# A batched 64x64 matrix product: half of seven result tiles leaves by another DMA queue, in three pieces

## The chip, the cores and the metric

The kernel runs on one core of a Trainium2 chip. A core has a matrix engine (TensorE, PE in the profile), a vector engine (VectorE, DVE), a scalar engine (ScalarE, ACT), a general-purpose engine (GpSimd, POOL) and an engine that mostly issues transfers (SyncE, SP). Transfers between the main memory (HBM) and the on-chip memory are run by 16 DMA engines; SyncE, ScalarE and GpSimd each have a DMA queue of their own (q1, q10 and q0 in the profile). The metric is the device time of one execution in microseconds; the median of 3 runs before the change is 134.86 us (134.75 to 134.9).

## The reference

```python
def setup_inputs():
    return {
        "a": np.random.randn(1024, 64, 64).astype(np.float32),
        "b": np.random.randn(1024, 64, 64).astype(np.float32),
    }

def reference(a, b):
    return np.matmul(a, b).astype(np.float32)
```

There are 1024 independent products of two 64x64 matrices. Each input is 16.8 MB and so is the output.

## The kernel before

The 1024 products are worked off in 16 tiles of 64 products; t is the number of the tile, from 0 to 15. For one tile, b is 1.05 MB and the result is 1.05 MB. The matrix a is read in pieces for two tiles at a time; s is the number of such a piece, from 0 to 7.

The loads are these. `load_b(t)` (L93) issues one transfer, by SyncE for even t and by ScalarE for odd t, into one of 3 buffers. `load_a(s)` (L69) issues three transfers by GpSimd that convert to bf16 on the way (`a_sb`, 0.52 MB read each) and one by SyncE (`a_raw`, 0.52 MB). The first piece of a is loaded by SyncE and ScalarE.

The computation of a tile has these steps. `regroup(s)` (L99) puts the piece of a into another order on VectorE. `transpose(s, j)` (L115) turns it on TensorE and copies the result out on ScalarE (`at_sb`, L123). `spread(t)` (L128) makes the block-diagonal operand from it with four VectorE copies (`at_bd`, L133). `cast(t)` (L140) makes bf16 of the tile of b on VectorE (`b_bf`, L144). `multiply(t)` (L158) runs 64 matrix products in two halves and copies each half from PSUM into `o_sb` (L177), four copies a half: all on ScalarE, except that in odd tiles two of the eight are VectorE's. `o_sb` has 8 buffers, the PSUM tile `o_ps` has 2.

The result of tile t is handed to `store(t)` one tile later, after `multiply(t + 1)`. For t from 0 to 13 this is one transfer of the whole tile by GpSimd (L166); tile 14 goes out in two halves by SyncE and tile 15 in four quarters by SyncE and ScalarE.

The order of the work is written out by hand in the main loop (L229 to L256), and every engine and every DMA queue follows it in order. In the round of tile t the loop calls, in this order: `spread(t+1)`, `cast(t+1)`, `load_b(t+3)`, in some even rounds `load_a`, `transpose`, then `multiply(t)`, `regroup`, `transpose`, and `store(t-1)`. An engine that waits before it issues a transfer does nothing else meanwhile; for ScalarE this means that its copies (L123, L177) stand behind the issue of an odd tile of b.

One thing is not in the source but in the built program. Every transfer that SyncE or ScalarE issues signals its landing on one of eight semaphores, H0 to H7, taken in turn over both engines in program order; GpSimd's transfers have eight of their own. Before a transfer is issued, its engine waits until the transfer that last used the same semaphore has landed, unless another wait has made that sure already. So the ninth such transfer waits for the first, besides what its data and its buffer make it wait for.

Of the kernel before, what the change touches and what calls it, by code (L numbers as in the profile page):

```python
# [13 lines left out]
def kernel(  # L14
# [14 lines left out]
    nc = tc.nc  # L29
# [12 lines left out]
    o_v = out.rearrange("(t gh x) (mo w) n -> t (x mo) gh (w n)", gh=8, x=8, w=4)  # L42
# [19 lines left out]
    held = {}  # L62

    def store_queue(t, lo):
        if t < n_t - 2:
            return nc.gpsimd
        return nc.scalar if t == n_t - 1 and lo % 4 == 0 else nc.sync
# [90 lines left out]
    def multiply(t):  # L158
        at_bd = bd_tiles[t % N_BD][:].rearrange("p j g wl h mo -> p j g (wl h mo)")
        at_bd = at_bd.bitcast(bf16).rearrange("p j g (c u) -> p j g c u", u=2)  # L160
        b_bf = bbf_tiles.pop(t)
        last = t == n_t - 1
        o_sb = o_pool.tile([128, 8, 2, 2, 64], fp32, name="o_sb")

        def put(lo, n):
            store_queue(t, lo).dma_start(  # L166
                out=o_v[t, :, lo : lo + n, :],
                in_=o_sb[:, lo : lo + n].rearrange("p gh j wl n -> p (gh j wl n)"),
            )

        def evacuate(o_ps, gh, n, copies):

            for par in range(2):
                for wl in range(2):
                    src = o_ps[64 * wl : 64 * wl + 64, :, par, :, :]
                    dst = o_sb[64 * par : 64 * par + 64, gh : gh + n, :, wl, :]
                    copies[2 * par + wl](dst, src)  # L177

        for half in range(2):
            if not last:  # L180
                o_ps = o_psum.tile([128, 4, 2, 2, 64], fp32, name="o_ps")
            for g8 in range(8):
                if last and g8 % 4 == 0:
                    o_ps = t_psum.tile([128, 2, 2, 2, 64], fp32, name="at_ps")
                g = 8 * half + g8
                gl = (g8 % 4 if last else g8) // 2
                for j in range(2):
                    for u in range(2):
                        nc.tensor.matmul(  # L189
                            o_ps[:, gl, g % 2, j, :],  # L190
                            at_bd[:, j, g, :, u],
                            b_bf[:, g, 64 * u : 64 * u + 64],
                            start=(u == 0),
                            stop=(u == 1),
                        )
                if last and g8 % 4 == 3:
                    copy = nc.scalar.copy if g8 == 3 else nc.vector.tensor_copy
                    evacuate(o_ps, g // 4 * 2, 2, [copy] * 4)
            if not last:
                copies = [nc.scalar.copy] * 4  # L200
                if half and t % 2:
                    copies[2:] = [nc.vector.tensor_copy] * 2
                evacuate(o_ps, 4 * half, 4, copies)
        if last:
            held[t] = [lambda q=q: put(2 * q, 2) for q in range(4)]
        else:
            whole = t < n_t - 2
            held[t] = [lambda q=q: put(q, 8 if whole else 4) for q in ([0] if whole else [0, 4])]

    with tc.manual_schedule():  # L210
# [18 lines left out]
        for t in range(n_t):  # L229
            s, half = t // 2, t % 2  # L230
            if t + 1 < n_t:
                spread(t + 1)
                cast(t + 1)
            if t + B_AHEAD < n_t:
                load_b(t + B_AHEAD)
            if half == 0 and 0 < s < n_s - 1 - A_AHEAD:
                load_a(s + 1 + A_AHEAD)
            if half == 0 and 0 < s < n_s - 1:
                transpose(s + 1, 1)
            multiply(t)  # L240
            if t == 0:
                regroup(1)
                load_a(A_AHEAD)
                load_a(A_AHEAD + 1)
                transpose(1, 0)
                transpose(1, 1)
            elif t == 1:
                regroup(2)
            elif half == 0 and s + 2 < n_s:
                regroup(s + 2)  # L250
            if half == 1 and s + 2 < n_s:
                transpose(s + 2, 0)
            if t >= HOLD - 1:
                store(t - HOLD + 1)
# [32 lines left out]
```

## Time and profile before

| | us |
|---|---|
| median of 3 runs | 134.86 |
| span of the profiled execution | 133.1 |
| VectorE busy | 94.5 (71%) |
| ScalarE busy | 87.8 (66%) |
| TensorE busy | 65.7 (49%) |
| GpSimd busy | 33.7 (25%) |
| mean DMA rate by bytes written | 338 GB/s |
| HBM traffic over the span | 33.55 MB read, 16.78 MB written, 378 GB/s |

The profile covers one execution, whose span from the first to the last instruction is 133.1 us. The difference of 1.76 us to the median lies outside this span. Where a transfer converts to bf16, the rate counts the bytes written, which are half of those read. A page of the profile gives the busy time of the engines in 40 slices of the span; further views list the chain of work that ended last, the instructions in order of time, and for a transfer the time from its issue to its landing.

### The profile page before, as it was taken

Reading aid. Unit: us, or ns where it says so; the run is one execution under the profiler, and the core shown is the slowest. Engines: PE = TensorE matmul, PEld = TensorE weight load, DVE = VectorE, ACT = ScalarE, POOL = GpSimd, SP = SyncE. Lnnn points to the kernel's source line nnn. Section 1 sums busy time; section 2 is a strip of 40 time slices with the busy share of each in tenths; the row PEclk is TensorE's granted clock in tenths of the full one; section 3 lists DMA queues with packets and bytes.
Section 4 is the critical chain, followed back from the end, with each engine's and each line's share of the span. In section 5 each row is a group of like instructions: output and inputs, shape, how many; then the busy total and the mean of one; then the engine's idle time right before and its main releaser. Section 6 shows DMA issues by size and latency. Waiting matters only on the chain.

```text
span 133.1 us, 2837 instructions
## 1 busy us (share of the span) xinstructions
PE 65.7 (49%) x1152; PEld 62.7 (47%) x1152; DVE 94.5 (71%) x120; ACT 87.8 (66%) x161; POOL 33.7 (25%) x43
## 2 busy tenths in 40 slices
PE   0005504990068386059519672986199361776000
PEld 0005304980068275058509562975199360766000
DVE  5930299208999719598999699969999994978100
ACT  3134505899128999919899759696969987099600
POOL 8981000420082072143144022203020410210000
PEclk9999999999559999968996875579756985556855
DMA  3999999999999999999999999999999999999991
GB/s 75 367 332 311 307 312 279 278 307 326 328 307 402 316 322 334 393 385 401 318 282 365 402 397 356 308 307 387 395 396 387 393 396 391 402 403 402 380 339 41
DMA packets 19021, 45.01 MB, mean 338 GB/s; under 512 B 1088, under 2 KB 3136, under 8 KB 19008
## 3 DMA queue, kind: packets, MB, share of 16 engines
q0 software_dynamic: 6832, 20.19, 50.2%
q1 hardware_dynamic: 7120, 14.68, 30.5%
q10 hardware_dynamic: 5056, 9.96, 19.8%
q8 instruction: 9, 0.15, 0.4%
q14 instruction: 4, 0.03, 0.1%
HBM read 33.55 MB, written 16.78 MB: 378 GB/s over the span
## 4 chain that ended last, share of the span: by engine, by line
DMA 54%; DVE 18%; ACT 13%; issue 4%; PE 3%; SPq 1%; DVEq 0%; ACTq 0%
DMA b_sb<-in_b_dram 54%; ACT o_sb L177 9%; DVE at_bd L133 9%; DVE b_bf L144 4%; DVE o_sb L177 3%; PE at_ps L120 2%; ACT at_sb L123 2%; ACT b_bf L144 1%; PE o_ps L189 1%; DVE a_bf L108 1%; SPq L90 1%; DVE a_bf L111 1%; ACT b_bf L151 1%; SPq L96 0%; DVEq L133 0%
## 5 line engine op out<-in xcount | busy, mean ns | idle before, releaser
L177 ACT COPY o_sb<-o_ps 64x512 f32<-64x512 f32 x106 | 61.6, 581 | 9.5 <-PE o_ps L189 8.2
L189 PEld LDWEIGHTS <-at_bd 128*128 128x128 bf16 x1024 | 42.5, 113 | 39.7 <-DVE b_bf L144 26.8
L189 PE MATMUL o_ps<-b_bf,at_bd 128*128 128x64 bf16 x960 | 41.2, 213 | 36.0 <-DVE b_bf L144 25.1
L133 DVE COPY at_bd<-at_sb 32x1024 f32<-32x1024 f32 x64 | 46.6, 728 | 13.6 <-ACT at_sb L123 11.8
L120 PE MATMUL at_ps<-identity,a_bf 128*128 128x128 f32 x128 | 22.5, 350 | 19.3 <-ACT a_bf L105 11.4
L166 POOL DMA_DIRECT2D out_dram<-o_sb x14 | 16.3, 1166 | 55.4 <-ACT at_sb L123 23.0
L120 PEld LDWEIGHTS at_ps<-identity,a_bf 128*128 128x128 f32 x128 | 20.7, 190 | 19.4 <-issue 19.4
L144 DVE CAST b_bf<-b_sb 128x2048 bf16<-128x2048 f32 x14 | 17.5, 1249 | 10.0 <-DMA b_sb<-in_b_dram 9.8
L123 ACT COPY at_sb<-at_ps 128x512 f32<-128x512 f32 x32 | 17.4, 590 | 9.9 <-PE at_ps L120 7.6
L73 POOL DMA_DIRECT2D a_sb<-in_a_dram x21 | 13.3, 650 | 27.3 <-DVE a_bf L108 20.4
L177 DVE COPY o_sb<-o_ps 64x512 f32<-64x512 f32 x14 | 9.7, 690 | 0.3
L108 DVE COPY a_bf<-a_sb 128x3072 bf16<-128x3072 bf16 x7 | 7.4, 1059 | 0.0
L105 ACT CAST a_bf<-o_sb 128x1024 bf16<-128x1024 f32 x2 | 2.1, 1044 | 5.3 <-DMA o_sb<-in_a_dram 5.3
L111 DVE CAST a_bf<-a_raw 128x1024 bf16<-128x1024 f32 x7 | 4.8, 683 | 0.0
L144 ACT CAST b_bf<-b_sb 128x2048 bf16<-128x2048 f32 x1 | 1.9, 1897 | 4.1 <-DMA b_sb<-in_b_dram 4.1
L177 DVE COPY o_sb<-at_ps 64x256 f32<-64x256 f32 x8 | 3.4, 422 | 1.3 <-PE at_ps L189 1.2
L105 DVE CAST a_bf<-o_sb 128x1024 bf16<-128x1024 f32 x2 | 2.6, 1296 | 2.4 <-DMA o_sb<-in_a_dram 2.3
L189 PE MATMUL at_ps<-b_bf,at_bd 128*128 128x64 bf16 x64 | 3.6, 242 | 1.0 <-DVE at_bd L133 1.0
L217 DVE MEMSET at_bd<- 128x4096 f32 x1 | 3.5, 3472 | 0.8 <-issue 0.8
L151 ACT CAST b_bf<-b_sb 128x512 bf16<-128x512 f32 x2 | 1.1, 615 | 4.3 <-DMA b_sb<-in_b_dram 4.3
L177 ACT COPY o_sb<-at_ps 64x256 f32<-64x256 f32 x8 | 2.9, 367 | 0.1
L214 ACT ACT_TABLE_LOAD x1 | 1.3, 1283 | 2.3 <-issue 2.3
(12 smaller groups left out, 6.1 us busy)
## 6 DMA issues: line engine op xcount, KB each, us to landing
out_dram<-o_sb POOLq DMA_DIRECT2D x14, 1024.0 KB, 22.3
a_sb<-in_a_dram POOLq DMA_DIRECT2D x21, 256.0 KB, 16.4
a_raw<-in_a_dram SPq DMA_DIRECT2D x7, 512.0 KB, 19.1
o_sb<-in_a_dram SPq DMA_DIRECT2D x2, 512.0 KB, 6.2
o_sb<-in_a_dram ACTq DMA_DIRECT2D x2, 512.0 KB, 7.3
out_dram<-o_sb SPq DMA_DIRECT2D x2, 512.0 KB, 7.4
out_dram<-o_sb SPq DMA_DIRECT2D x2, 256.0 KB, 7.7
out_dram<-o_sb ACTq DMA_DIRECT2D x2, 256.0 KB, 5.9
```

The costliest lines, as they stand in the source:

```text
L73: nc.gpsimd.dma_start(out=a_sb[:, h, :, :].rearrange("p v k -> p (v k)"), in_=a_v[s, h])
L105: copy(a_bf[:, :, h, :], a_sb[h].rearrange("p (v k) -> p v k", v=16))
L108: nc.vector.tensor_copy(a_bf[:, :, 0:3, :], cast_sb[:].rearrange("p h v k -> p v h k"))
L111: nc.vector.tensor_copy(a_bf[:, :, 3, :], raw[:])
L120: nc.tensor.transpose(at_ps[:, vo, :], a_cols[:, 4 * vo + 2 * j + wl, :], identity[:])
L123: nc.scalar.copy(at_tiles[s][:, j, :, wl, :, :], at_ps[:].rearrange("p vo (g mp) -> p g mp vo", mp=4),)
L133: nc.vector.tensor_copy(bd[rows, :, :, :, h, :].rearrange("p j g wl mo -> p j (g wl) mo"), at_tiles[t // 2][rows, :, half, :, :, :].rearrange(
L144: (nc.vector.tensor_copy if t else nc.scalar.copy)(b_bf[:], b_sb[:])
L166: store_queue(t, lo).dma_start(out=o_v[t, :, lo : lo + n, :], in_=o_sb[:, lo : lo + n].rearrange("p gh j wl n -> p (gh j wl n)"),)
L177: copies[2 * par + wl](dst, src)
L189: nc.tensor.matmul(o_ps[:, gl, g % 2, j, :], at_bd[:, j, g, :, u], b_bf[:, g, 64 * u : 64 * u + 64], start=(u == 0), stop=(u == 1),)
L217: nc.vector.memset(bd_tiles[0][:], 0.0)
```

## The change

For tiles 4 to 10 the single transfer by GpSimd becomes one by GpSimd of the second half of the tile (`put(4, 4)`, 0.52 MB), and three by SyncE of the first half (`put_rows(0, 4)`). These three split the 128 partitions into 112, 16 - r and r, with r = t - 3 from 1 to 7. Each partition has 4 runs of 1 KB in the half, so that the small pieces have 4 KB to 60 KB. Nothing else is changed; the whole diff:

```diff
@@ -201,7 +201,16 @@
                 if half and t % 2:
                     copies[2:] = [nc.vector.tensor_copy] * 2
                 evacuate(o_ps, 4 * half, 4, copies)
-        if last:
+        def put_rows(lo, n):
+            for first, end in ((0, 112), (112, 131 - t), (131 - t, 128)):
+                nc.sync.dma_start(
+                    out=o_v[t, first:end, lo : lo + n, :],
+                    in_=o_sb[first:end, lo : lo + n].rearrange("p gh j wl n -> p (gh j wl n)"),
+                )
+
+        if 4 <= t <= 10:
+            held[t] = [lambda: put(4, 4), lambda: put_rows(0, 4)]
+        elif last:
             held[t] = [lambda q=q: put(2 * q, 2) for q in range(4)]
         else:
             whole = t < n_t - 2
```

The order of the instructions of TensorE, VectorE and ScalarE stays as it was. SyncE issues 21 transfers more, and as these take part in the turn of the eight semaphores, the waits of what follows change too. In the built program, SyncE's and ScalarE's transfers from the load of b for tile 8 on are these ("s4" is the SyncE half of result tile 4 and has three transfers; b8 is the tile 8 of b; ar6 and ar7 are `a_raw` of the pieces 6 and 7; in brackets what the transfer waits for apart from its own data and its buffer, "x landed" being the last user of the same semaphore):

```
before                       after
SP  b8  H2                   SP  b8  H2
                             SP  s4  H3, H4, H5
SP  ar7 H3                   SP  ar7 H6
ACT b9  H4                   ACT b9  H7
                             SP  s5  H0, H1 [b7 landed], H2 [b8 landed]
SP  b10 H5                   SP  b10 H3 [112 rows of s4 landed]
                             SP  s6  H4, H5
ACT b11 H6                   ACT b11 H6 [ar7 landed]
                             SP  s6  H7 [b9 landed]
                             SP  s7  H0, H1, H2 [the pieces of s5 landed]
SP  b12 H7                   SP  b12 H3 [b10 landed]
                             SP  s8  H4, H5 [two pieces of s6 landed]
ACT b13 H0 [ar6 landed]      ACT b13 H6 [b11 landed]
                             SP  s8  H7 [the last piece of s6 landed]
                             SP  s9  H0, H1, H2 [the pieces of s7 landed]
SP  b14 H1                   SP  b14 H3 [b12 landed]
                             SP  s10 H4, H5 [two pieces of s8 landed]
ACT b15 H2                   ACT b15 H6 [b13 landed]
                             SP  s10 H7 [the last piece of s8 landed]
```

Some further waits on the same semaphores are for transfers that landed long before and are left out here.

## The prediction

> **What bounds the kernel now.** I read the DMA rows of the page first, then the chain of waits, then each engine in order of time between 70 and 126 us. The page:
>
> ```profile
> span 133.1 us, 2837 instructions
> DMA  3999999999999999999999999999999999999991
> GB/s 75 367 332 311 307 312 279 278 307 326 328 307 402 316 322 334 393 385 401 318 282 365 402 397 356 308 307 387 395 396 387 393 396 391 402 403 402 380 339 41
> ```
>
> The 16 DMA engines are busy in every slice but the first and the last. Where no transfer converts on the way the rate is about 0.39 MB/us. The HBM bytes (33.55 + 16.78 MB) do not change, so less time can only come from the last slices or from better balance; more time comes if work arrives too late to keep them busy. The chain of waits, in the place that matters:
>
> ```profile
> 68.57 1.24 DVE b_bf L144
> ...
> 69.88 18.85 DMA b_sb<-in_b_dram
> ...
> 88.82 0.09 DVE b_bf L144
> ```
>
> At 69.88 SyncE issues b10 (tile 10 of b), as soon as VectorE has read b7 out of the buffer; it lands at 88.73, and the cast that needs it starts at 88.82. So b10 sets the end at this place: every microsecond by which it lands later is a microsecond here. VectorE in order of time shows how much of such a delay is made good:
>
> ```profile
> 88.82 1.23 DVE L144 CAST b_bf<-b_sb 128x2048 bf16<-128x2048 f32 x1 [1.23 <-DMA b_sb<-in_b_dram]
> ...
> 107.42 3.21 DVE L133 COPY at_bd<-at_sb 32x1024 f32<-32x1024 f32 x4
> 112.54 1.23 DVE L144 CAST b_bf<-b_sb 128x2048 bf16<-128x2048 f32 x1 [1.92 <-DMA b_sb<-in_b_dram]
> ```
>
> From 88.82 to 110.63 (107.42 + 3.21) it works back to back; then it waits 1.92 us for b14. The slack after b10 is that, and 1.4 us on ScalarE near the end: ScalarE waits 4.28 us for b15 until 116.54, with half 0 of tile 14 ready to be copied at about 115, and without the wait VectorE's last copies (120.30 + 3.49 = 123.8, plus a little) would end the computing at about 124.1 instead of 125.5.
>
> **The change, part by part.**
>
> *GpSimd.* Seven issues carry half as much. One took 0.90 to 1.86 us, mean 1.17; GpSimd is busy 25%, and its idle time before these issues ended with ScalarE's copies. I take 0; if this cover were gone, seven halves would be worth 7 x 0.6 = 4.1 us either way.
>
> *SyncE's issues.* 21 more. The shortest issue of an L166 transfer on SyncE took 0.38 us, so 8 us in all, against the queue's waits of 57 us between 40 and 100 us. I take 0 for the issuing itself; uncovered it would be 8 us.
>
> *Bytes and packets.* How three queues share the engines is shown from 56 to 60 us, when q0 moves a result, q10 and q1 a tile of b:
>
> ```profile
> q0 software_dynamic: 194, 0.73, 47.6%
> q10 hardware_dynamic: 198, 0.40, 27.7%
> q1 hardware_dynamic: 198, 0.41, 26.4%
> ```
>
> Packets are equal in number, bytes are not: the queues take turns by packet, and GpSimd's result packets are of 4 KB, those of b of 2 KB. SyncE's results go in packets of 1 KB (its last stores are 834 packets of 0.81 MB from 126.8 to 129 us, at 367 GB/s, where q0 alone has 404 GB/s from 116 to 119). The 7 halves of 0.524 MB cost at most 3.67/0.367 - 3.67/0.404 = 0.9 us of DMA time more. While computing is late, this is hidden, 0; if the DMA engines set the end, it is +0.9.
>
> *b10 behind the results.* This is the main term. SyncE's queue is served in order. After b8 it held ar7 and b10, and now s4, ar7, s5 and b10. b8 landed at 75.9 (issued at 57.97, 17.9 to landing). From there to b10's landing at 88.73 the queue moved 0.524 + 1.049 MB in 12.86 us, 122 GB/s beside both other queues. The two halves add 1.049 MB: at the same rate 8.6 us. From below: b9 lands at 81.1 as it did, ScalarE's next load is held back (next part), GpSimd's results are halved, and a SyncE queue with half of 390 GB/s needs 2.62/0.195 = 13.4 us, b10 at 89.3, +0.6. From above: with packets of 1 KB the halves go at half the rate of b, 1.049/0.061 = 17.2 us. I take 8.6: the two effects work against each other, and the total (2.62 MB on q1, some 1.5 MB on q10, over 4 MB on q0, together over 8 MB at 0.39) makes at least 21 us from 75.9, if q0 with its larger packets is served first. So b10 lands near 97.
>
> *The waits of the semaphores.* b10 is no longer issued at 69.88: the third piece of s5, in front of it, waits for b8 (75.9), and b10 itself for the 112 rows of s4. That is earlier than its turn in the queue comes, so no more than the term above. Worse placed is ScalarE, whose issue of b11 now waits for ar7, behind which its copies stand:
>
> ```profile
> 77.23 0.02 ACT L96 MOVE_SHAPE b_sb<-in_b_dram  x1 [1.58 <-DVE b_bf L144]
> ...
> 78.99 4.74 ACT L177 COPY o_sb<-o_ps 64x512 f32<-64x512 f32 x8
> ```
>
> ar7 landed at 79.2 (issued at 59.74, 19.5 to landing). With 0.524 MB of s4 in front, at 122 GB/s, it lands 4.3 us later, at 83.5; with 1 KB packets 8.6 later, at 87.8. ScalarE stands still from 77.2 to then, 6 to 11 us; the copies of tile 8 begin at 85 to 90, those of tile 9 end by 96 to 101, and `multiply(9)` waits for a free PSUM tile. Whoever waits further on is `cast(10)`, which waits for b10 anyway. So this price lies under the term above and adds 0; if b10 came in time, it would itself cost 6 less the slack.
>
> *b12 to b15.* Each now waits until the tile two before has landed (b12 for b10). Before, b12 was issued 5.6 us before b10 landed. Between b10 and b12 the queues have two SyncE halves, b12, b13 and three GpSimd halves to move, 4.7 MB, 12.1 us at 0.39, where VectorE needs 11.65 (88.82 to 100.47). I give up half of the slack before b14 for it and keep 1.0 us of the 1.92; both ends are 0 and 1.9.
>
> *The end.* The last store took 5.7 us from 125.52, as 1 MB stores from before were still moving. With fewer results outstanding I take 3.5; it lies between 5.7 and the 2.5 that its 0.26 MB plus the shortest visible latency make, an estimate from the last rows. Gain 2.2.
>
> The Trainium skill speaks against the small pieces. "DMA: Bandwidth & Descriptors", "Rules for kernel authors", says to coalesce, as transfers under 64 KB are mostly overhead, and "Anatomy of one DMA" gives some 2.0 us of fixed cost a transfer. By the page the 14 small pieces would cost up to 28 us, were they one after another; by the rows 0, as queues take turns and latencies overlap. The same page, "Why a DMA increments its semaphore by 16 and not by 1", says that such a transfer uses as many engines as divide its rows, up to 16, the lowest-numbered ones. By that, engine 15 moves 28 KB less and engine 0 28 KB more of some 3.1 MB each, an estimate of 1.2 us if engine 15 always came last. No row of before tells the engines apart.
>
> **The sum.** + 8.6 (b10) - 1.0 (wait for b14) - 1.4 (wait for b15) - 2.2 (last store) = + 4.0. Span 133.1 + 4.0 = 137.1; with the 1.76 around it, 138.9.
>
> **The rivals.**
>
> *A: the loads come in time and the end comes earlier.* b10 lands by 92, as q1 gets half of the engines. Then fewer results wait in q0 when the last tile is computed, and the last 6 us (126 to 132, DMA shares 1.08, 0.85 and 0.13) are filled: 6 x (1 - 0.69) = 1.9 us, less 0.9 for small packets, -1.0, to 133.9; with better balance 133.3. For it speaks that results land 26 to 30 us after their issue in the middle, so q0 has much to give away. Against it: the turns by packet. It decides while b10 is late by less than the slack and the last store's gain, about 4 us.
>
> *B: delay and relief cancel.* b10 late by 4.5 us: within 0.3 us of 134.9. The same rows; a narrow place between A and the forecast.
>
> *C: packets of 1 KB are fully penalised.* b10 is 12 us late or more (17.2 at most), b12 and b14 find no slack: 12 - 1.4 - 2.2 = + 8.4, 143.3, and more. For it the equal packet counts, against it that q0 and q10 run empty.
>
> *D: the change does not do what it says.* The built program has all 21 transfers, so no chance.
>
> **How the numbers follow.** The forecast, slower by 1.5 to 7.5 us (136.4 to 142.4), has 0.62; C 0.07; A 0.20; B has 0.11, of which 0.05 lies within 0.2% (0.27 us), about what a measurement of this kernel tells from no change, 0.05 is slower and 0.01 goes to faster. Faster 0.21, same 0.05, slower 0.74. The range goes from A's far side at 133.5 to 143.3, the mild side of C, and leaves out some 0.1 to 0.2. The forecast's own range is 136.4 to 142.4.
>
> **What would show it.** b10's landing near 97 and its cast then; ScalarE without work from 77 to 84 or later, released by a transfer of `a_raw`; SyncE's queue waiting on tiles of b; VectorE back to back after `cast(10)`; the last store landing in under 4 us; DMA slices under 9 near the end. It is wrong if b10 lands before 92, or if VectorE waits much longer than 2 us after it: then the turn of the queues, or the waits of b12 to b15, were mis-sized.

## The result, and the profile after

The change makes the kernel slower: 139.25 us (median of 4 runs, 138.85 to 139.6) against 134.81 us (134.65 to 134.9). The ratio is 1.0329, with a 95% interval of 1.0309 to 1.035. Medians, here and below, take in all runs of a kernel, while ratios leave out those that were disturbed and came out longer; where the few bytes are cut by partitions, below, this makes 0.5 to 1.4 us. The span of the profiled execution grew from 133.1 to 137.4 us, by 4.3 us.

The page of the changed kernel, its span and the two DMA rows:

```profile
span 137.4 us, 2873 instructions
...
DMA  3999999999999999999999999999999999999885
GB/s 103 383 320 308 305 297 274 290 309 329 319 367 347 304 327 392 388 394 337 285 348 399 348 253 363 403 325 292 380 339 289 385 392 298 348 392 385 318 284 185
```

As before, the DMA row is full almost to the end. But from 90 us on the rate falls below 340 GB/s again and again (325, 292, 339, 289, 298), where before it stayed between 380 and 403 from 90 to 126 us. The engines are counted as busy and move less.

The chain of waits of the changed kernel (start, duration, what), at the place that the prediction spoke of and from there on:

```profile
58.86 23.50 DMA out_dram<-o_sb
...
82.49 15.29 DMA b_sb<-in_b_dram
...
97.87 1.24 DVE b_bf L144
...
99.18 11.40 DMA b_sb<-in_b_dram
...
110.79 13.47 DMA b_sb<-in_b_dram
```

A SyncE half of tile 4 (s4, issued from 58.86 us on) holds back the issue of b10 to 82.49 us; it was 69.88 before. b10 lands at 97.78 (88.73 before), and its cast starts 9.05 us later than before. The other two loads of the chain are b13, issued when that cast has freed its buffer, and b15, issued at 110.79 us (101.78 before) after b13 had landed at 110.58. The landing is not alone there: the cast that frees b15's buffer ends at 110.28 and ScalarE's own copies at 110.57.

VectorE in order of time (start, busy time, engine, line, operation, and in brackets the idle time before it and what ended that):

```profile
97.87 1.23 DVE L144 CAST b_bf<-b_sb 128x2048 bf16<-128x2048 f32 x1 [7.27 <-DMA b_sb<-in_b_dram]
...
109.05 1.23 DVE L144 CAST b_bf<-b_sb 128x2048 bf16<-128x2048 f32 x1
...
119.11 1.23 DVE L144 CAST b_bf<-b_sb 128x2048 bf16<-128x2048 f32 x1
```

These are `cast(10)`, `cast(12)` and `cast(14)`. From 97.87 us to `cast(14)` VectorE does not wait any more: `cast(14)` has lost the 1.92 us of waiting that it had before. It is 6.57 us late where `cast(10)` was 9.05 late.

ScalarE in order of time, first the issue of b11, then the end:

```profile
85.85 0.02 ACT L96 MOVE_SHAPE b_sb<-in_b_dram  x1 [9.50 <-DMA a_raw<-in_a_dram]
...
117.88 3.55 ACT L177 COPY o_sb<-o_ps 64x512 f32<-64x512 f32 x6 [0.65 <-PE o_ps L189]
124.34 1.14 ACT L151 CAST b_bf<-b_sb 128x512 bf16<-128x512 f32 x2 [2.90 <-DVE at_bd L133]
...
133.30 0.38 ACTq L166 DMA_DIRECT2D out_dram<-o_sb  x1
```

And the same stretch at the end, before the change:

```profile
108.71 3.55 ACT L177 COPY o_sb<-o_ps 64x512 f32<-64x512 f32 x6 [0.47 <-PE o_ps L189]
116.54 1.14 ACT L151 CAST b_bf<-b_sb 128x512 bf16<-128x512 f32 x2 [4.28 <-DMA b_sb<-in_b_dram]
```

b15 was issued 9.01 us late, is 13.47 instead of 14.68 us under way and lands at 124.26 us, 7.80 us late. ScalarE's copies of tile 13 end at 121.43 instead of 112.26 us (start plus busy time), and it still waits 2.90 us for b15, 4.28 before (the row names VectorE, the chain of waits names the load). So its cast of b15 is 7.80 us late, and the last issue of a store 7.78 us (125.52 before). From there the last transfer lands 2.97 us later, at 136.27 us; before it was 6.24 us (131.76). 7.78 - 3.27 leaves 4.5 us, and 0.2 us less lies behind the last landing: the 4.3 us.

### The profile page after: what moved, and what is told of

Same layout as the page of the kernel before. It is cut to its first block, busy times and chain, and to the rows that moved or that the text cites. A ratio compares the mean times of both kernels' runs of the same rounds, so it can differ in the third digit from the quotient of the medians.

```text
span 137.4 us, 2873 instructions
## 1 busy us (share of the span) xinstructions
PE 65.3 (48%) x1152; PEld 62.0 (45%) x1152; DVE 91.8 (67%) x120; ACT 88.0 (64%) x161; POOL 32.0 (23%) x43
## 4 chain that ended last, share of the span: by engine, by line
DMA 71%; ACT 11%; DVE 7%; PE 3%; issue 3%; SPq 1%; ACTq 0%; DVEq 0%
DMA b_sb<-in_b_dram 54%; DMA out_dram<-o_sb 17%; ACT o_sb L177 8%; DVE b_bf L144 2%; DVE at_bd L133 2%; PE at_ps L120 2%; ACT at_sb L123 2%; ACT b_bf L144 1%; PE o_ps L189 1%; SPq L90 1%; DVE o_sb L177 1%; DVE a_bf L108 1%; ACT b_bf L151 1%; DVE a_bf L111 0%; SPq L96 0%
## 5 line engine op out<-in xcount | busy, mean ns | idle before, releaser
L189 PEld LDWEIGHTS <-at_bd 128*128 128x128 bf16 x1024 | 42.0, 112 | 48.8 <-DVE b_bf L144 25.7
L133 DVE COPY at_bd<-at_sb 32x1024 f32<-32x1024 f32 x64 | 45.3, 708 | 16.2 <-ACT at_sb L123 14.4
L166 POOL DMA_DIRECT2D out_dram<-o_sb x14 | 15.2, 1088 | 66.8 <-ACT o_sb L177 32.7
L73 POOL DMA_DIRECT2D a_sb<-in_a_dram x21 | 12.8, 623 | 25.3 <-DVE a_bf L108 19.1
L96 ACT MOVE_SHAPE b_sb<-in_b_dram x8 | 0.5, 64 | 12.3 <-DMA a_raw<-in_a_dram 9.5
L108 DVE COPY a_bf<-a_sb 128x3072 bf16<-128x3072 bf16 x7 | 6.7, 953 | 0.0
L105 DVE CAST a_bf<-o_sb 128x1024 bf16<-128x1024 f32 x2 | 1.6, 812 | 4.1 <-DMA o_sb<-in_a_dram 4.1
```

The lines of the kernel that those rows point to most:

```text
L73: nc.gpsimd.dma_start(out=a_sb[:, h, :, :].rearrange("p v k -> p (v k)"), in_=a_v[s, h])
L105: copy(a_bf[:, :, h, :], a_sb[h].rearrange("p (v k) -> p v k", v=16))
L108: nc.vector.tensor_copy(a_bf[:, :, 0:3, :], cast_sb[:].rearrange("p h v k -> p v h k"))
L133: nc.vector.tensor_copy(bd[rows, :, :, :, h, :].rearrange("p j g wl mo -> p j (g wl) mo"), at_tiles[t // 2][rows, :, half, :, :, :].rearrange(
L166: store_queue(t, lo).dma_start(out=o_v[t, :, lo : lo + n, :], in_=o_sb[:, lo : lo + n].rearrange("p gh j wl n -> p (gh j wl n)"),)
L189: nc.tensor.matmul(o_ps[:, gl, g % 2, j, :], at_bd[:, j, g, :, u], b_bf[:, g, 64 * u : 64 * u + 64], start=(u == 0), stop=(u == 1),)
```

## The experiments

The theory: b10 stands in SyncE's queue behind the halves, lands late, and this lateness less some slack is the loss. Against it stood the waits of the semaphores (and with them ScalarE's stall), the splitting and the small pieces in themselves, and a loss in proportion to the bytes, wherever they go. All kernels compute everything; they differ in who issues which transfer. In the diffs "-" is the changed kernel, if nothing else is said. Times are medians of the runs, ratios stand to the kernel before with 95% intervals.

**One piece instead of three.** This leaves the bytes in the queue and takes away 14 transfers, with them the turns of the semaphores that made ScalarE wait for `a_raw`.

```diff
-            for first, end in ((0, 112), (112, 131 - t), (131 - t, 128)):
+            for first, end in ((0, 128),):
```

> The SyncE half of tiles 4 to 10 goes out in one transfer instead of three. The same bytes stand in SyncE's queue at the same places, but with 7 transfers instead of 21 the turn of the eight semaphores no longer makes b11 wait for a_raw, nor b10, b12 to b15 for a load two tiles before. Queue theory (b10 stands behind two halves in 1 KB packets): b10 still lands at 95 to 99 and the time stays at 137 to 140 us. Semaphore theory (the waits make the loss): b10 lands near 89 and the time falls to 134 to 135.5 us.

139.59 us; 1.0362 [1.0334, 1.039]. The chain of waits, and VectorE at `cast(10)`:

```profile
70.90 27.70 DMA b_sb<-in_b_dram
```

```profile
98.69 1.23 DVE L144 CAST b_bf<-b_sb 128x2048 bf16<-128x2048 f32 x1 [10.82 <-DMA b_sb<-in_b_dram]
```

Here b10 is issued at 70.90 us, 1 us later than before the change, and ScalarE waits only 0.98 us at the issue of b11 (it stands 10.52 us at that of b13 instead, until `cast(10)` has freed its buffer). Still b10 lands at 98.60 us, as late as with the three pieces: what was a wait before the issue is now time in the queue. Neither the semaphores nor the number of pieces cost anything that shows; the halves in front of b10 are what is left.

**Both halves by GpSimd.**

```diff
-            held[t] = [lambda: put(4, 4), lambda: put_rows(0, 4)]
+            held[t] = [lambda: put(4, 4), lambda: put(0, 4)]
```

> Tiles 4 to 10 go out in two halves, both by GpSimd. Both theories: splitting alone costs nothing, 134.3 to 135.5 us; if GpSimd's seven further issues (0.9 us each) or its own semaphores matter, above 135.5.

134.89 us (10 runs); 1.0004 [0.9991, 1.0017]. VectorE at `cast(10)` and `cast(14)`:

```profile
88.28 1.23 DVE L144 CAST b_bf<-b_sb 128x2048 bf16<-128x2048 f32 x1 [1.46 <-DMA b_sb<-in_b_dram]
...
111.28 1.23 DVE L144 CAST b_bf<-b_sb 128x2048 bf16<-128x2048 f32 x1 [1.51 <-DMA b_sb<-in_b_dram]
```

The loads land as before or a little earlier (`cast(14)` by 1.3 us). Splitting a result in two costs nothing; the loss comes with SyncE's queue.

**No load of b behind the halves, and its control.** In the first kernel the halves leave by SyncE in one piece, and b9 to b15 all go by ScalarE. The second has only the new placing of b, with the results as in the kernel before.

```diff
-        queue = nc.scalar if t % 2 else nc.sync
+        queue = nc.scalar if t % 2 or t > 8 else nc.sync
```

> As the one-piece kernel, but b of tiles 9 to 15 is loaded by ScalarE alone, so that no load of b stands behind a result in a queue. Queue theory: b10 lands at 87 to 91 and the time is 133.5 to 136 us, clearly below the one-piece kernel. If it is the share of 1 KB and 4 KB packets on the engines and not the place in the queue, it stays within 1 us of the one-piece kernel.

> The control for the run with the halves in one piece and b9 to b15 by ScalarE (135.9 us, +0.8%): the same placing of b9 to b15, with the results as before the change. If a SyncE half costs time only through the load of b behind it, this kernel stands within 0.5 us of that one: 135.4 to 136.4, and its cast(10) near 89.7 us as well. If the halves still cost something of their own there (bytes, packets, the a_raw behind them), this kernel is faster than that one by more than 0.5 us: 134.0 to 135.3. If moving b to ScalarE's queue is itself a loss that the halves partly paid back by relieving GpSimd's queue, it is slower: above 136.5.

With halves 135.9 us; 1.0077 [1.0062, 1.0092]. The control without halves 138.72 us; 1.0292 [1.0265, 1.032]. `cast(10)` with halves:

```profile
89.75 1.23 DVE L144 CAST b_bf<-b_sb 128x2048 bf16<-128x2048 f32 x1 [2.55 <-DMA b_sb<-in_b_dram]
```

ScalarE in the control (for "ACTq", the issue of a transfer, the second number is the time until the issue was done):

```profile
83.27 4.93 ACTq L96 DMA_DIRECT2D b_sb<-in_b_dram  x1
...
90.21 5.82 ACTq L96 DMA_DIRECT2D b_sb<-in_b_dram  x1
...
96.07 1.07 ACT L123 COPY at_sb<-at_ps 128x512 f32<-128x512 f32 x2 [3.13 <-issue]
...
105.77 5.84 ACTq L96 DMA_DIRECT2D b_sb<-in_b_dram  x1
...
111.65 1.07 ACT L123 COPY at_sb<-at_ps 128x512 f32<-128x512 f32 x2 [3.12 <-issue]
```

With the halves on SyncE but no b behind them, `cast(10)` is 0.9 us late instead of 9 or 10. That part of the theory holds. By the time alone, 135.9 looked as if the halves still cost 0.8%. The control says otherwise, and of its three expectations the third came true. Moving b to ScalarE alone loses 3.8 us. The five issues from b11 to b15 take 3.3 to 5.8 us each (0.70 before), and ScalarE's copies stand idle for 2.1 to 3.4 us of each, 13.9 us in all. Onto that the halves *bring* 2.8 us (138.72 to 135.9): b13 lands at 107.93 instead of 111.31 us, and ScalarE's copies lose only 8.13 us, to three of the issues (2.75, 2.18 and 3.20). So half a result on SyncE is worth something, measured against this control, where no load of b stands behind it. The change pays more for b10 than it gets from this.

**A smaller part of each result.** The SyncE part is one piece of one eighth or one quarter of the columns of the seven tiles; GpSimd takes the rest.

```diff
-            for first, end in ((0, 112), (112, 131 - t), (131 - t, 128)):
+            for first, end in ((0, 128),):
...
-            held[t] = [lambda: put(4, 4), lambda: put_rows(0, 4)]
+            held[t] = [lambda: put(1, 7), lambda: put_rows(0, 1)]   # one eighth
+            held[t] = [lambda: put(2, 6), lambda: put_rows(0, 2)]   # one quarter
```

> As the one-piece kernel, but SyncE sends one eighth of the columns of tiles 4 to 10 (0.13 MB, all 128 partitions, one transfer) and GpSimd seven eighths. Queue theory, by bytes: 0.26 MB in front of b10 at 122 GB/s make its cast 2.1 us late, at 90 to 92 us, and the slack takes most of it: 134.5 to 136.5 us. If the order of the queue has no part in it, nothing ties the time to the bytes, and it stays near the one-piece kernel (over 138).

> The same with one quarter of the columns (0.26 MB a tile). Queue theory: 0.52 MB in front of b10, its cast 4.3 us late, at 92 to 95 us, and a time between that of the eighth and that of the half: 135.5 to 138 us.

One eighth: 139.49 us; 1.0343 [1.0317, 1.0369]. One quarter: 139.44 us; 1.0323 [1.0263, 1.0383]. Both expectations missed: the time hardly depends on the bytes. By the words of the first one a time over 138 us speaks against the queue; the casts show that b10 is late behind the small part all the same, and the loads after it too. VectorE's casts with one eighth, then DMA share and GB/s (the last two numbers) by stretches of the same run, then the casts with one quarter:

```profile
93.11 1.23 DVE L144 CAST b_bf<-b_sb 128x2048 bf16<-128x2048 f32 x1 [5.37 <-DMA b_sb<-in_b_dram]
...
106.11 1.23 DVE L144 CAST b_bf<-b_sb 128x2048 bf16<-128x2048 f32 x1 [1.42 <-DMA b_sb<-in_b_dram]
...
119.53 1.23 DVE L144 CAST b_bf<-b_sb 128x2048 bf16<-128x2048 f32 x1 [3.27 <-DMA b_sb<-in_b_dram]
```

```profile
120.00:124.00 4.00, 3.19 (x60) 3.19 (x61) 3.86 (x6) 2.38 (x5) 0.53 (x1) 0.50 0.51 201
124.00:126.00 2.00, 1.05 (x21) 0.89 (x19) 1.94 (x4) 1.95 (x4) 0.81 (x1) 0.50 0.30 104
```

```profile
95.99 1.23 DVE L144 CAST b_bf<-b_sb 128x2048 bf16<-128x2048 f32 x1 [8.76 <-DMA b_sb<-in_b_dram]
...
120.79 1.23 DVE L144 CAST b_bf<-b_sb 128x2048 bf16<-128x2048 f32 x1 [3.21 <-DMA b_sb<-in_b_dram]
```

How late the casts are against before (88.82, 100.47, 112.54), with the bytes of the two parts in front of b10:

| kernel | MB in front | cast(10) | cast(12) | cast(14) | span |
|---|---|---|---|---|---|
| one eighth | 0.26 | +4.3 | +5.6 | +7.0 | 137.1 |
| one quarter | 0.52 | +7.2 | +6.9 | +8.3 | 137.6 |
| half, three pieces (the change) | 1.05 | +9.1 | +8.6 | +6.6 | 137.4 |
| half, one piece | 1.05 | +9.9 | +9.4 | +7.4 | 138.1 |
| half, three pieces, only tiles 4 and 5 (below) | 1.05 | +13.5 | +13.4 | +11.5 | 142.6 |

For b10 the bytes count, though not in proportion: the prediction's rate would give 2.1, 4.3 and 8.6 us. Afterwards the rows cross. With a small part the later loads fall further behind (VectorE waits 3.27 us for b14 again); with a half they catch up. At `cast(14)` the first four stand at +6.6 to +8.3. In the run with one eighth the DMA engines even run at half their time and less from 120 to 126 us: the last load has landed by 121.3, and little is computed yet to be stored. That it is the fuller GpSimd queue that delays b12 and b14 there is argued from this order and from the control above, not shown. A rival stands beside it: b12 is behind the small parts of tiles 6 and 7 as well, and is issued at 84.96 us (83.09 before), when SyncE is done with issuing these.

**Only tiles 4 and 5.** These two halves stand in front of b10; the other five go back to GpSimd. This kernel is the last row of the table.

```diff
-        if 4 <= t <= 10:
+        if 4 <= t <= 5:
```

> Only tiles 4 and 5 have their first half sent by SyncE, in the three pieces of the change; both stand in front of b10. Queue theory: b10 lands at 95 to 99 as in the changed kernel, the delay is carried to the end, and 2 of 7 tiles cost most of the whole: 137 to 140 us. Rival (each half costs its share, by packets or issues): 2/7 of the loss of 4.4 us, about 136.1 us.

144.35 us; 1.0701 [1.0677, 1.0724]. VectorE at `cast(10)`, and the stretches from 126 us on:

```profile
102.35 1.23 DVE L144 CAST b_bf<-b_sb 128x2048 bf16<-128x2048 f32 x1 [13.73 <-DMA b_sb<-in_b_dram]
```

```profile
126.00:128.00 2.00, 0.47 (x18) 0.38 (x13) 1.50 (x3) 1.98 (x4) 0.00 (x0) 0.97 0.47 180
128.00:130.00 2.00, 1.86 (x32) 1.70 (x32) 1.93 (x3) 1.91 (x5) 0.86 (x1) 0.50 0.00 0
```

Two halves cost 9.4 us, all seven 4.4. The rival of a loss in proportion to the halves (136.1) falls, and so does the size that the theory gave (137 to 140). The two in front of b10 do all the damage, and the five others give back 5.1 us of it. With whole results in GpSimd's queue beside it, b10 lands at 102.26 instead of 97.78 us, although the same bytes stand in front of it.

**Only tiles 10 to 13.** Their halves are issued behind b14, the last load of b on SyncE.

```diff
-        if 4 <= t <= 10:
+        if 10 <= t <= 13:
```

> Only tiles 10 to 13 have their first half sent by SyncE, in the three pieces of the change; all stand behind b14, SyncE's last load. Queue theory: no load of b stands behind them, 134 to 135.6 us. Rival (each half costs its share): 4/7 of 4.4 us, about 137.3 us.

136.09 us; 1.0078 [1.0048, 1.0108]: 0.5 us above the range of the theory and 1.2 below the figure of the rival, nearer to the theory but a miss. `cast(14)` and ScalarE's cast of b15:

```profile
112.54 1.23 DVE L144 CAST b_bf<-b_sb 128x2048 bf16<-128x2048 f32 x1 [2.06 <-DMA b_sb<-in_b_dram]
```

```profile
117.65 1.14 ACT L151 CAST b_bf<-b_sb 128x512 bf16<-128x512 f32 x2 [5.24 <-DMA b_sb<-in_b_dram]
```

Nothing is late up to `cast(14)`, the same 112.54 as before; b15 on ScalarE's queue is then 1.1 us late. Four halves behind the loads cost 1.2 us, two in front of b10 9.4.

**Few bytes, cut by partitions.** GpSimd stores 112 partitions of the whole tile, and SyncE the last 16, one eighth of the bytes: first in three uneven pieces, then in three parts of columns with all 16 partitions, then in one transfer.

```diff
-            held[t] = [lambda: put(4, 4), lambda: put_rows(0, 4)]
+            held[t] = [lambda: put_rows(nc.gpsimd, 0, 112, 0, 8)] + [
+                lambda lo=lo, n=n: put_rows(nc.sync, 112, 128, lo, n) for lo, n in ((0, 3), (3, 3), (6, 2))
+            ]
```

This is the second kernel (`put_rows` has gained the queue and the partitions as arguments); the third has ((0, 8),), and the first splits the 16 partitions as (112, 120), (120, 131 - t), (131 - t, 128).

> GpSimd sends 112 partitions of the whole tile for tiles 4 to 10, SyncE the last 16 partitions in three pieces: 21 SyncE transfers as in the change, but 0.13 MB a tile instead of 0.52. The waits of b10 (for b8) and of b12 to b15 (for the load two tiles before) stay; only ScalarE's wait for a_raw goes. Queue theory: b10 lands at 88 to 91, time 134 to 136 us. Semaphore theory: time 137 us or more.

> The same bytes as in the few-bytes kernel, 112 partitions by GpSimd and the last 16 partitions by SyncE in three transfers, but each of the three has all 16 partitions and a part of the columns, instead of 8, 8 - r and r partitions or the like. If the few-bytes kernel lost 8 us because its pieces fall on few of the 16 DMA engines, this one takes 134 to 136 us; if the semaphores' waits (b10 for b8, b12 for b10, b14 for b12) or GpSimd's 112 partitions are the cause, it stays above 139 us.

> 112 partitions of tiles 4 to 10 by GpSimd, the last 16 partitions by SyncE in one transfer (0.13 MB a tile, all 16 partitions, 7 SyncE transfers). Nothing waits on a semaphore for a late load now, and only 0.26 MB stand in front of b10. Queue theory: b10's cast at 89 to 92 us, time 134 to 136 us; the remaining 5 us of the even few-bytes kernel then came from the semaphores' waits, which matter once the queue is short. If it stays above 138 us, GpSimd's transfer of 112 partitions is to blame, and the few-bytes kernels say nothing on the queue.

> The even few-bytes kernel once more, on the same chip as the one-transfer kernel: 138 to 141 us as before, clearly above the one-transfer kernel if the semaphores' waits make the difference.

Uneven pieces: 143.17 us (141.25 to 144.23); 1.0515 [1.047, 1.0561]. Parts of columns: 140.1 (138.03 to 141.33); 1.0289 [1.0219, 1.0358], and again: 138.21 (137.97 to 139.51); 1.0257 [1.0205, 1.0309]. One transfer: 143.81 (142.18 to 145.6); 1.0612 [1.0537, 1.0686]. VectorE in the kernel with parts of columns:

```profile
93.05 1.23 DVE L144 CAST b_bf<-b_sb 128x2048 bf16<-128x2048 f32 x1 [4.46 <-DMA b_sb<-in_b_dram]
...
106.91 1.23 DVE L144 CAST b_bf<-b_sb 128x2048 bf16<-128x2048 f32 x1 [2.68 <-DMA b_sb<-in_b_dram]
```

The first three missed the 134 to 136 us that the theory gave: few bytes in SyncE's queue do not cost little here. The kernel with parts of columns agrees with one eighth of the columns above in `cast(10)` (93.05 and 93.11). By the ratios the other two are 3 to 5 us slower than it, with the same bytes on each queue. The expectation of the third would put this on GpSimd's transfer of 112 partitions, but the kernel with parts of columns has the same transfer. The waits of the semaphores are not the cause either, as the kernel with one transfer has fewer of them and is the slowest, where the last expectation would have had it faster. What it is stays open, and no reading here rests on these two.

None of the kernels is faster than the one before the change; both halves by GpSimd equals it.

## Why the prediction was right, and where not

**b10 behind the halves (+8.6): right.** Measured +9.05. From b8's landing (about 75.96 us, just before its cast at 76.05) to b10's (97.78) SyncE's queue moved the 2.62 MB of s4, `a_raw`, s5 and b10 in 21.8 us, 0.120 MB/us, where the step had taken 0.122. The half in one piece, both halves by GpSimd, and b moved off the queue show that it is this and neither the splitting nor the semaphores. The step was right for the change, but its rule (bytes by a fixed rate) does not carry to other kernels. A quarter of the bytes in front cost half of the delay (1.84 MB in 17.1 us with one eighth, 0.107 MB/us), and with tiles 4 and 5 alone the same 2.62 MB took 25.9 us, 0.101. The prediction let slower small packets and the relief of GpSimd's queue cancel without a figure for either; that they left the rate of before almost as it was is in part luck.

**The waits of the semaphores (0): right.** ScalarE's stand at b11 was 9.50 us, forecast as 6 to 11, released by `a_raw`, forecast for 83.5 to 87.8 us and landed at 85.76. It lies under the wait for b10; with one piece it is not there any more, and nothing is gained.

**b14 and b15 (-1.0 and -1.4): the step that failed.** The sum took both off one after the other. VectorE's wait for b14 did go, from 1.92 to 0 us, but the end does not lie behind it: the chain runs from `cast(10)` by the buffers over b13 to b15, and b15 is still the last to come. So the -1.0 should not have been in the sum. The 1.4 was what would be gained if the wait for b15 went altogether and VectorE set the end. That did not happen: 2.90 us of the wait are left. What the chain gains there is b15's shorter time under way, 1.21 us; that the wait shrank by 1.38, so close to 1.4, is chance.

**The last store (-2.2): right in kind, too small.** The store that was issued last took 5.74 us before, as the step read it, and 2.97 after. But before the change another store landed after it (issued at 124.31 us, landed at 131.76), so the stretch from the last issue to the last landing shrank by 3.27 us. The two misses nearly cancel, and so far the sum is luck: forecast 8.6 - 1.0 - 1.4 - 2.2 = +4.0; measured 9.05 - 0.04 (to the issue of b15) - 1.21 (b15 under way) - 0.02 (to the last issue) - 3.27 - 0.2 = +4.3.

**GpSimd's and SyncE's issues, packets and pieces (0): right for the pieces, not seen in full for the bytes.** Three pieces (139.25) and one (139.59) take the same time. By the Trainium skill ("DMA: Bandwidth & Descriptors", "Rules for kernel authors") small transfers are to be coalesced; this case's runs show no price for 14 of them, where they travel beside other work. The 2.0 us that the prediction quotes from the same page are given there for transfers issued by GpSimd, and these pieces are SyncE's. The step on the packets held lateness and DMA rate apart, and the changed kernel's trace does not: see the last section.

**The relief of GpSimd's queue: mis-sized.** The prediction gave it a figure in the last store alone, and in the term of b10 let it cancel against small packets. The runs show 5.1 us for the five halves of tiles 6 to 10, and 2.8 us for all seven where no b stands behind them.

**The rivals.** A (b10 by 92 us) falls with b10 at 97.78. Its mechanism, relief, is real, but does not outweigh the queue. B needed b10 late by 4.5 us and a gain of the same size; with one eighth b10 was late by 4.3 us and the kernel lost 4.6, as the loads after it gained nothing back. C needed 12 us, and b10 was late by 9.05. Without the relief what C feared is nearer: with tiles 4 and 5 alone the two halves made b10 13.5 us late, 0.078 MB/us for their 1.049 MB, between the forecast's 0.122 and C's 0.061, and the kernel came out at 144.35 us, where C was put.

## What to carry to other kernels

A store that is put in front of a load on the same in-order queue delays that load and all that waits for it, even when it is small (0.26 MB made b10 4.3 us late); if results are to be spread over queues, put them where no load that the end depends on follows: four halves behind the loads cost 1.2 us here, two in front of b10 9.4. Add up slacks only along one chain: two waits on two engines do not both come off the end. When part of a move is undone to find its cost, measure the control with that part alone too, since here the undone part had a cost of its own that was larger than the effect sought.

## What the runs showed of the hardware

A full DMA row is not a full rate. The DMA queues from 92 to 96 us (packets, MB, share of the 16 engines' time), before the change:

```profile
q0 software_dynamic: 240, 0.92, 59.2%
q1 hardware_dynamic: 240, 0.49, 31.9%
q10 hardware_dynamic: 88, 0.18, 12.1%
```

and after it:

```profile
q10 hardware_dynamic: 357, 0.72, 64.8%
q1 hardware_dynamic: 257, 0.45, 40.4%
```

Both stretches are full, with shares that sum to over 100%. Before, results leave beside the loads, and 1.59 MB move in 4 us. After, GpSimd's queue is empty, loads travel almost alone, and 1.17 MB move; a byte on q1 takes 1.4 times as long (40.4% / 0.45 MB against 31.9% / 0.49). Over the stretch from 76 to 120 us 14.93 MB moved instead of 16.65. The 1.72 MB less, at the 0.378 MB/us of before, are 4.5 us, as much as the loss. This agreement holds for the changed kernel alone: by the same count the kernel with one piece moved 15.45 MB, 3.2 us less, and its span grew by 5.0 us; with one eighth it moved 16.41 MB, 0.6 us less, and the span grew by 4.0. Packets of 1 KB are not enough to cause it: the kernel with halves and b on ScalarE had as many small packets in that stretch (3762 under 2 KB, against 3539 after the change) and moved 16.53 MB. So lateness of computing can show as a lower rate, when stores run out beside the loads, and not only as idle DMA engines; with one eighth, and with tiles 4 and 5 alone, it does show as idle engines near the end (the stretches above). Why loads alone are slower, no run here tells.

A queue of ScalarE held back a third load. In the control every issue of b from b11 on was done when the load two before it had landed (b11's at 80.37, the landing of b9; b12's at 88.20, b10 landed at 87.84; b13's at 96.03, b11 at 95.69), and the engine's copies stood behind it. In the kernel with halves and b on ScalarE it is the same for b11 to b14. It was seen on this queue with loads of 1.05 MB. On SyncE's queue before the change it is not a plain count of transfers: b10's issue was done at 70.58 us, though b8, two before it with an `a_raw` of 0.52 MB between, landed only at 75.88. What is counted was not tried.
